# Making the combined forms of x earlier in a SwiGLU feed-forward of a two-layer trunk

## The chip, the cores and the metric

One Trainium2 chip, one core. The metric is the device time of one execution of the whole program in microseconds; the profile is of one execution on that core.

## What is computed

The trunk has two layers over x (512 tokens x 1024). Each layer runs: feed-forward, mixer (an mLSTM in the first layer, a gated MLP in the second), feed-forward, gated embedding; after each of them stands `x = LayerNorm(alpha * x + sublayer(x))`. So there are four feed-forwards, and the change touches these alone:

```python
D_MODEL = 1024; SEQ = 512; DEPTH = 2; FFN_HIDDEN = 2816

def swiglu_ffn(x, w_gu, w_d):
    g, u = jnp.split(x @ w_gu, 2, axis=-1)
    return (jax.nn.silu(g) * u) @ w_d

for i in range(DEPTH):
    x = layer_norm(DN_ALPHA * x + 0.5 * swiglu_ffn(x, ffn1_wgu[i], ffn1_wd[i]), ln_g[i, 0], ln_b[i, 0])
    # ... the mixer of this layer and its norm ...
    x = layer_norm(DN_ALPHA * x + 0.5 * swiglu_ffn(x, ffn2_wgu[i], ffn2_wd[i]), ln_g[i, 2], ln_b[i, 2])
    # ... the gated embedding and its norm ...
```

## The kernel before

Every float32 operand of a product is held as two parts, a high one (`xh`, `whi`, `fhi`) and the rest (`xl`, `wlo`, `flo`), and each product is three matmuls: high by high (L388), and the two mixed ones (L389, L390). ScalarE makes a high part with a copy (L275, L393, L942), VectorE the rest with a subtraction (L284, L394, L945); for some weights the rest is made by ScalarE and an accumulating DMA from GpSimd's queue (L281, L282).

A feed-forward goes through its 22 blocks of 128 hidden columns in six chunks, `FFN_CHUNKS = [2, 4, 4, 4, 4, 4]`. In the chunks c = 0 and 1 the up products are plain: for each of the 2n values of i one product of all eight blocks of x with 128 columns (tile `fps`; the first three, `sup`, are begun before x is complete), then `sg` (ScalarE, SiLU) for even i and `h` (VectorE, L1193) for odd i. From chunk 2 on (`UP_FROM = 2`) the up products use a seven-product scheme (Strassen's, in Winograd's form): four products of quarters of x and of the weights become seven products, r = 0 to 6, of sums of quarters (tile `ups`). Meanwhile the previous chunk's down products run in the same scheme (class `Group`, tile `gps`, added to `xt` by VectorE at L762 and L764).

The seven products need sums of x's quarters, and `UpForms` makes them once in each feed-forward by a list of ten steps, of which `formed.step()` runs the next. A quarter is half of x's blocks by half of the tokens. The steps, in order, with the names of the trace:

1. `x22`: high and low part of a quarter added into two half tiles `x_a` (L1001, two instructions)
2. `x_f`, tile b: the same of a second quarter (L1001)
3. `t3`: b = x_a - b (L1013, two)
4. `x_f`, tile c: the same of a third quarter, which lies in the last 256 tokens (L1001)
5. c = b + c (L1027)
6. `split_t2`: `t_whi` by ScalarE (L393), `t_wlo` by VectorE (L394)
7. `t1`: x_a = x_a - c (L1017, two)
8. `split_t1`: two `t` by ScalarE (L393), two by VectorE (L394)
9. `x21`: `x_d` (L1001, two), of a quarter in the last 256 tokens
10. `t4`: x_d = x_d - c (L1038, two)

The first three need the first 256 tokens alone. What is left, the split of t3 into `xh` and `xl` and that of t4 into `t_f`, is made by `formed.last` in the first products of chunk 2.

There is no scheduler: each engine runs its instructions in the order in which the program writes them, and waits on semaphores where data or a buffer is not there. Weights go through rings of buffers that `W.release()` refills (ScalarE's copy, VectorE's or the DMA's rest, SyncE's next load). After the first feed-forward, chunk 0 and the first values of i in chunk 1 also hold `run_affine`, two VectorE instructions over all of `xt` (L756, L757).

In chunk 2 the product r = 2 adds onto the bank of r = 0, and r = 4 onto that of r = 2. So each of them waits until ScalarE has copied the bank (`take`, L1086, tile `us`).

Of the kernel before, what the change touches and what calls it, by code (L numbers as in the profile page):

```python
# [357 lines left out]
def hybrid_trunk(ctx: ExitStack, tc, x, p, ln_g, ln_b, ffn1_wgu, ffn1_wd, ffn2_wgu, ffn2_wd,  # L358
# [9 lines left out]
    def stage_pool(name, bufs=1):  # L368
        return tc.tile_pool(name=name, bufs=bufs, side="left", reuse_waits="tile")
# [30 lines left out]
    def up_bank(name, hold=False):  # L400

        i = next(i for i in up_order if i not in up_held)
        up_order.remove(i)
        up_order.append(i)
        bank = ps_up.tile([P, 512], F32, name=name, tag=f"up{i}")
        if hold:
            up_held.add(i)
            return i, bank
        return bank
# [60 lines left out]
    FFN_CHUNKS = [2, 4, 4, 4, 4, 4]  # L470
    LAST = len(FFN_CHUNKS) - 1
    UP_FROM = 2
    FORM_AT = 2
    turn_p = []

    def ffn_weights(wgu, wd, name, ple=False):
# [233 lines left out]
    class Norm:  # L710
# [18 lines left out]
        def prepare(self, t):  # L729
            mv = small.tile([P, 2], F32, name="mv", tag="mv")  # L730
            vec.bn_aggr(mv, self.st[t])
            rs = small.tile([P, 2], F32, name="rs", tag="rs")
            vec.tensor_scalar(rs[:, 0:1], mv[:, 1:2], EPS, None, op0=OP.add)
            pool.tensor_tensor(rs[:, 1:2], rs[:, 0:1], eps_pow, op=OP.pow)
            self.rs[t] = mv[:, 0:1], rs[:, 1:2]
# [115 lines left out]
    def up(ps, w, t0=0, t1=SEQ, hooked=()):  # L851

        for kb in range(KB):
            if kb in hooked:
                run_hook()
            mm3(ps[:, t0:t1], [a[:, kb] for a in w], xs(kb, t0, t1), kb == 0, kb == KB - 1)

    def up_staged(first=False):

        banks = [up_bank("sup") for _ in range(3)]  # L860
        ws = []

        def low_last(w, ps, t0, t1):

            for k0, kbs in ((0, range(KB // 2)), (1, range(KB // 2, KB))):
                for kb, a in ([(kb, a) for a in w for kb in kbs] if first else [(kb, a) for kb in kbs for a in w]):
                    mm(ps[:, t0:t1], a[:, kb], xh[:, kb, t0:t1], start=kb == 0 and a is w[0], stop=False)
            if not first and not t0:
                run_hook()
            for kb in range(KB):  # L870
                mm(ps[:, t0:t1], w[0][:, kb], xl[:, kb, t0:t1], start=False, stop=kb == KB - 1)

        for i, ps in enumerate(banks):
            w = W.take()
            ws.append(w)
            if i:
                up(ps, w, 0, 256, (((0,), (2, 7)) if first else ((), (0, 3)))[i - 1])
                continue
            if not first:
                run_hook()  # L880
            low_last(w, ps, 0, 256)
        low_last(ws[0], banks[0], 256, SEQ)
        for ps, w in zip(banks[1:], ws[1:]):
            up(ps, w, 256, SEQ)
        return banks
# [224 lines left out]
    def ffn(layer, k, rows, late, prepare=None):  # L1110
        with stage_pool("forms", 2) as fpool, stage_pool("quarters", Q_BUFS) as qpool, \
                stage_pool("hpool", 2) as hpool, stage_pool("tforms") as tpool:
            name = (layer, k)
            W.open_raw(name, qpool, Q_BUFS)
            banks = deque(up_staged((layer, k) == (0, 0)))

            def project():
                if banks:
                    return banks.popleft()
                ps = up_bank("fps")  # L1120
                up(ps, W.take())
                return ps

            def halves(a):
                return a[:, :SEQ], a[:, SEQ:]

            group, hs, norm, formed = None, [], None, None

            def up_products(c, n, h):
                nonlocal norm  # L1130
                for s in range(7 * n // 2):
                    b, r = s // 7 * 2, s % 7
                    if r == 0:
                        pair = UpPair(formed, None if h is None else h[:, b:b + 2])
                    pair.product(r)
                    W.clock += 1
                    group.add()
                    if r == 5 and h is None:
                        pair.parts = [W.spare(name).rearrange("p (b t) -> p b t", b=2) for _ in range(2)]
                        hs.extend([a[:, e] for a in pair.parts] for e in range(2))  # L1140
                    if r == 6:
                        pair.gated(1, pair.part[2], pair.part[3])
                    pair.take(r)
                    group.finish_form()
                    W.lows()
                    if c == UP_FROM and s in formed.last:
                        formed.last[s]()
                    W.release()
                    pair.gate(r)
                    W.form_ahead(3)  # L1150
                    if s % 2:
                        group.product()
                        W.release(kind="rows")
                        group.form(True)
                    if s == 12 and h is not None:
                        next_group = Group(h, fpool)
                        next_group.form()
                    if c == LAST and b == n - 2:
                        if r == 2:
                            W.open("rowsx", late, 1)  # L1160
                        elif r == 4:
                            norm = Norm(layer, k)
                group.add()
                W.lows()
                return next_group if h is not None else None

            for c, n in enumerate(FFN_CHUNKS):
                if c < LAST:
                    h = hpool.tile([P, 4, SEQ], F32, name="h", tag="h")[:, :n]
                elif prepare is not None:  # L1170
                    prepare()
                if c == UP_FROM - 1:
                    formed = UpForms(tpool, late)
                W.apart = c >= UP_FROM
                if c >= UP_FROM:
                    next_group = up_products(c, n, h if c < LAST else None)
                    if c < LAST:
                        next_group.form()
                    group.add()
                    group = next_group  # L1180
                for i in range(2 * n if c < UP_FROM else 0):
                    b = i // 2
                    ps = project()
                    W.clock += 2
                    if group is not None and i:
                        group.add()
                    if i % 2 == 0:
                        sg = tmp_tile("sg")
                        sca.activation(sg, ps, AF.Silu)
                        W.release()  # L1190
                    else:
                        hf = h[:, b] if c < LAST else tmp_tile("hf")
                        vec.scalar_tensor_tensor(hf, sg, 0.5, ps, op0=OP.mult, op1=OP.mult)  # L1193
                        if c == LAST:
                            hs.append(halves(W.spare(name)))
                            split(*hs[b], hf)
                        W.release()
                        run_hook()
                    if group is not None and i < 7:
                        group.product()  # L1200
                        W.release(kind="rows")
                        group.form()
                    if c == 1 and i < 3:
                        run_affine()
                    if formed is not None and i >= FORM_AT:
                        formed.step()
                        formed.step()
                    if c and i == 6:
                        next_group = Group(h, fpool)
                        next_group.form()  # L1210
                if c < UP_FROM and c:
                    group = next_group
                    group.form()
                if c == UP_FROM - 1:
                    while formed.steps:
                        formed.step()
                if c == 0:
                    group = Group(h, fpool, c == 0)
                    group.form()
                    group.form()  # L1220
                if c == 0:
                    run_affine()
            W.apart = False
            return down(hs, False, norm, lazy=layer == 0, defer=prepare is not None)
# [727 lines left out]
```

## Time and profile before

| | us |
|---|---|
| median of 3 runs | 2213.9 |
| the runs | 2211.8, 2213.9, 2218.28 |
| the profiled execution | 2217.81 |
| its span, first to last instruction | 2216.1 |
| TensorE busy in it | 2179.8 (98%) |
| VectorE busy in it | 1762.2 (80%) |
| ScalarE busy in it | 1209.0 (55%) |
| mean granted TensorE clock | 0.994 |

Times within the trace count from the first instruction. Matmuls overlap, so TensorE's busy time is not TensorE at its peak; where it waits stands in the waits and the timeline. The four feed-forwards begin at about 0, 764, 1172 and 1800 us. Times of a place below are those of the second one, the second feed-forward of the first layer.

### The profile page before, as it was taken

Reading aid. Unit: us, or ns where it says so; the run is one execution under the profiler, and the core shown is the slowest. Engines: PE = TensorE matmul, PEld = TensorE weight load, DVE = VectorE, ACT = ScalarE, POOL = GpSimd, SP = SyncE. Lnnn points to the kernel's source line nnn. Section 1 sums busy time; section 2 is a strip of 40 time slices with the busy share of each in tenths; the row PEclk is TensorE's granted clock in tenths of the full one; section 3 lists DMA queues with packets and bytes.
Section 4 is the critical chain, followed back from the end, with each engine's and each line's share of the span. In section 5 each row is a group of like instructions: output and inputs, shape, how many; then the busy total and the mean of one; then the engine's idle time right before and its main releaser. Section 6 shows DMA issues by size and latency. Waiting matters only on the chain.

```text
span 2216.1 us, 32537 instructions
## 1 busy us (share of the span) xinstructions
PE 2179.8 (98%) x12821; PEld 1928.9 (87%) x12821; DVE 1762.2 (80%) x2532; ACT 1209.0 (55%) x1668; POOL 227.2 (10%) x279
## 2 busy tenths in 40 slices
PE   9999999999999999999999999999999999999998
PEld 8899997888888888999888799997888888899987
DVE  5898877777776779888886998877788768888887
ACT  3566656464646435666445466655345453666542
POOL 1011100011101101111000011110001100111100
PEclk9999999999999999999999999999999999999999
DMA  6587764376847435787532587753437733777651
GB/s 189 149 200 189 176 160 125 82 161 127 164 109 161 124 112 133 193 200 169 164 124 68 140 199 185 179 142 135 142 77 152 163 122 114 173 183 180 140 181 58
DMA packets 228097, 329.46 MB, mean 149 GB/s; under 512 B 9140, under 2 KB 163892, under 8 KB 227944
## 3 DMA queue, kind: packets, MB, share of 16 engines
q1 hardware_dynamic: 169104, 211.83, 29.1%
q0 software_dynamic: 52224, 100.86, 27.3%
q10 hardware_dynamic: 6616, 14.69, 2.0%
q8 instruction: 101, 1.65, 0.3%
q14 instruction: 52, 0.43, 0.1%
HBM read 224.58 MB, written 2.11 MB: 102 GB/s over the span
## 4 chain that ended last, share of the span: by engine, by line
PE 80%; DVE 10%; ACT 4%; issue 3%; DMA 2%; SPq 0%; POOL 0%; DVEq 0%; ACTq 0%; POOLq 0%
PE ups L388 8%; PE ups L390 8%; PE ups L389 8%; PE gps L388 7%; PE gps L389 7%; PE gps L390 7%; PE dps L389 2%; PE dps L390 2%; PE dps L388 2%; DVE wlo L284 2%; ACT whi L275 1%; PE gups L388 1%; PE vps L388 1%; PE zps L388 1%; PE zps L390 1%
## 5 line engine op out<-in xcount | busy, mean ns | idle before, releaser
L275 ACT ACTIVATE whi<-wbox 128x1024 fp32r<-128x1024 f32 x224 | 235.9, 1054 | 229.6 <-DVE wbox L141 101.6
L388 PE MATMUL ups<-xh,whi 128*128 128x256 f32 x1024 | 293.1, 286 | 11.5 <-ACT us L1086 11.5
L390 PE MATMUL ups<-xh,wlo 128*128 128x256 f32 x1024 | 293.0, 286 | 3.3 <-DMA wlo<-wbox 3.3
L389 PE MATMUL ups<-xl,whi 128*128 128x256 f32 x1024 | 292.6, 286 | 0.0
L275 ACT ACTIVATE whi<-wraw 128x1024 fp32r<-128x1024 f32 (+1 forms) x212 | 217.2, 1046 | 97.2 <-DVE wraw L119 22.6
L388 PE MATMUL gps<-whi,fhi 128*128 128x512 f32 x644 | 253.2, 393 | 1.3 <-ACT wlo L281 0.7
L390 PE MATMUL gps<-whi,flo 128*128 128x512 f32 x644 | 251.8, 391 | 1.7 <-DVE flo L945 1.7
L389 PE MATMUL gps<-wlo,fhi 128*128 128x512 f32 x644 | 252.3, 392 | 0.0
L282 POOL DMA_DIRECT2D wlo<-wbox x144 | 122.4, 850 | 1098.1 <-ACT wlo L281 772.4
L764 DVE TENSOR_TENSOR xt<-xt,gps 128x512 f32<-128x512 f32 x302 | 195.2, 681 | 26.7 <-PE gps L390 26.4
L388 PEld LDWEIGHTS ups<-xh,whi 128*128 128x128 f32 x1024 | 199.3, 195 | 15.4 <-ACT us L1086 13.2
L284 DVE TENSOR_TENSOR wlo<-wraw,whi 128x1024 fp32r<-128x1024 f32 (+1 forms) x140 | 167.7, 1214 | 46.0 <-ACT whi L275 45.2
L390 PEld LDWEIGHTS ups<-xh,wlo 128*128 128x128 f32 x1024 | 199.2, 195 | 4.1 <-DMA wlo<-wbox 4.1
L389 PEld LDWEIGHTS ups<-xl,whi 128*128 128x128 f32 x1024 | 199.4, 195 | 2.3
L275 ACT ACTIVATE whi<-wquarter 128x1024 fp32r<-128x1024 f32 (+1 forms) x140 | 135.3, 966 | 80.7 <-DVE wquarter L119 28.9
L281 ACT ACTIVATE wlo<-wbox 128x1024 fp32r<-128x1024 f32 x144 | 150.3, 1044 | 0.0
L390 PEld LDWEIGHTS gps<-whi,flo 128*128 128x128 f32 x644 | 120.9, 188 | 29.7 <-DVE flo L945 3.0
L388 PEld LDWEIGHTS gps<-whi,fhi 128*128 128x128 f32 x644 | 121.3, 188 | 25.8 <-ACT wlo L281 1.9
L389 PEld LDWEIGHTS gps<-wlo,fhi 128*128 128x128 f32 x644 | 121.3, 188 | 21.5
L945 DVE TENSOR_TENSOR flo<-h,fhi 128x512 fp32r<-128x512 f32 (+1 forms) x140 | 88.9, 635 | 57.5 <-ACT fhi L942 56.8
L290 DVE TENSOR_TENSOR wlo<-wquarter,whi 128x1024 fp32r<-128x1024 f32 x104 | 126.7, 1218 | 0.0
L388 PE MATMUL fps<-xh,whi 128*128 128x512 f32 x288 | 112.2, 390 | 0.0
(365 smaller groups left out, 5828.0 us busy)
## 6 DMA issues: line engine op xcount, KB each, us to landing
wlo<-wbox POOLq DMA_DIRECT2D x144, 512.0 KB, 5.7
wbox<-in_ffn_wgu_dram SPq DMA_DIRECT2D x128, 512.0 KB, 4.9
wquarter<-in_ffn_wd_dram SPq DMA_DIRECT2D x64, 512.0 KB, 5.9
wraw<-in_ml_w_in_dram SPq DMA_DIRECT2D x24, 1024.0 KB, 5.9
wlo<-wraw POOLq DMA_DIRECT2D x48, 512.0 KB, 6.4
wraw<-in_ffn_wgu_dram SPq DMA_DIRECT2D x15, 1024.0 KB, 5.9
wraw<-in_gm_w_in_dram SPq DMA_DIRECT2D x15, 1024.0 KB, 5.5
wraw<-in_ffn_wgu_dram SPq DMA_DIRECT2D x17, 512.0 KB, 4.6
```

Source lines behind the costliest of these rows:

```text
L275: self.nc.scalar.activation(hi[:, s], src[:, s], AF.Copy)
L281: self.nc.scalar.activation(lo[:, s], src[:, s], AF.Copy, scale=-1.0)
L282: self.nc.gpsimd.dma_start(lo[:, s], src[:, s], accum_op=OP.add)
L284: self.nc.vector.tensor_sub(lo[:, s], src[:, s], hi[:, s].bitcast(F32))
L290: self.nc.vector.tensor_sub(lo, src, hi.bitcast(F32))
L388: mm(ps, st[0], mv[0], start=start, stop=False, skip_group_check=more)
L389: mm(ps, st[0], mv[1], start=False, stop=False, skip_group_check=more)
L390: mm(ps, st[1], mv[0], start=False, stop=stop, skip_group_check=more)
L764: vec.tensor_add(dst, dst, ps)
L945: vec.tensor_sub(lo, src, hi.bitcast(F32))
```

## The change

`UpForms` is built at the start of chunk 0 instead of chunk 1, and one step is run at each i from 1 on, in both chunks. Chunk 0 has four values of i and so runs the steps 1 to 3; chunk 1 has eight and runs the steps 4 to 10, one each at i = 1 to 7. Before, chunk 1 alone ran them, two each at i = 2 to 6.

```diff
-    FORM_AT = 2
...
-                if c == UP_FROM - 1:
+                if c == UP_FROM - 2:
                     formed = UpForms(tpool, late)
...
                     if c == 1 and i < 3:
                         run_affine()
-                    if formed is not None and i >= FORM_AT:
-                        formed.step()
+                    if formed is not None and (i and c == UP_FROM - 2 or i > 0 and c == UP_FROM - 1):
                         formed.step()
```

One line is taken out near the head of the program, so lines behind it have a number lower by one in the changed kernel (L1001 becomes L1000). The instructions are the same ones; TensorE, GpSimd and SyncE have the same order as before. Three places in the second feed-forward show what moves.

VectorE in chunk 0, ahead of and behind its last `h`; before:

```order
L284 TENSOR_TENSOR wlo<-wquarter,whi 128x512
L284 TENSOR_TENSOR wlo<-wraw,whi 128x1024
L1193 SCALAR_TENSOR_TENSOR h<-sg,fps 128x512
L945 TENSOR_TENSOR flo<-h,fhi 128x256 x2
L756 TENSOR_TENSOR xt<-xt,gb 128x1024
L757 TENSOR_TENSOR xt<-xt,gb 128x1024
```

VectorE at the same place now (`x_f_7565` is tile b):

```order
L284 TENSOR_TENSOR wlo<-wquarter,whi 128x512
L1000 TENSOR_TENSOR x_a<-xh,xl 128x512 x2
L284 TENSOR_TENSOR wlo<-wraw,whi 128x1024
L1000 TENSOR_TENSOR x_f_7565<-xh,xl 128x1024
L1192 SCALAR_TENSOR_TENSOR h<-sg,fps 128x512
L1012 TENSOR_TENSOR x_f_7565<-x_a,x_f_7565 128x512 x2
L944 TENSOR_TENSOR flo<-h,fhi 128x256 x2
L755 TENSOR_TENSOR xt<-xt,gb 128x1024
L756 TENSOR_TENSOR xt<-xt,gb 128x1024
```

The steps 1, 2 and 3 have come in from chunk 1, one to each i.

VectorE at the end of chunk 1 and the start of chunk 2, around the last `h`; before (`x_f_7632` is tile c):

```order
L284 TENSOR_TENSOR wlo<-wbox,whi 128x1024
L1001 TENSOR_TENSOR x_d<-xh,xl 128x512 x2
L1038 TENSOR_TENSOR x_d<-x_d,x_f_7632 128x512 x2
L945 TENSOR_TENSOR flo<-h,fhi 128x512
L762 SCALAR_TENSOR_TENSOR xt<-xt,gps 128x512 x2
L1193 SCALAR_TENSOR_TENSOR h<-sg,fps 128x512
L284 TENSOR_TENSOR wlo<-wquarter,whi 128x1024
L945 TENSOR_TENSOR flo<-h,fhi 128x512
L394 TENSOR_TENSOR xl<-x_f_7631,xh 128x4x256
```

VectorE at the same place now (`x_f_7566` is tile c, `x_f_7565` tile b):

```order
L284 TENSOR_TENSOR wlo<-wbox,whi 128x1024
L1000 TENSOR_TENSOR x_d<-xh,xl 128x512 x2
L944 TENSOR_TENSOR flo<-h,fhi 128x512
L761 SCALAR_TENSOR_TENSOR xt<-xt,gps 128x512 x2
L1192 SCALAR_TENSOR_TENSOR h<-sg,fps 128x512
L284 TENSOR_TENSOR wlo<-wquarter,whi 128x1024
L1037 TENSOR_TENSOR x_d<-x_d,x_f_7566 128x512 x2
L944 TENSOR_TENSOR flo<-h,fhi 128x512
L394 TENSOR_TENSOR xl<-x_f_7565,xh 128x4x256
```

The subtraction of step 10 has gone behind the last `h`, ahead of the next `flo` and of `xl`.

ScalarE in chunk 1, around `t_whi` of step 6; before:

```order
L1189 ACTIVATE sg<-fps 128x512
L275 ACTIVATE whi<-wquarter 128x512
L275 ACTIVATE whi<-wraw 128x1024
L275 ACTIVATE whi<-wbox 128x1024
L942 ACTIVATE fhi<-h 128x256
L393 ACTIVATE t_whi<-x_f_7632 128x1024
L275 ACTIVATE whi<-wbox 128x1024
```

ScalarE at the same place now:

```order
L393 ACTIVATE t_whi<-x_f_7566 128x1024
L1188 ACTIVATE sg<-fps 128x512
L275 ACTIVATE whi<-wquarter 128x512
L275 ACTIVATE whi<-wraw 128x1024
L275 ACTIVATE whi<-wbox 128x1024
L941 ACTIVATE fhi<-h 128x256
L275 ACTIVATE whi<-wbox 128x1024
```

`t_whi` has gone ahead of the `sg` of i = 4; on VectorE c = b + c (step 5) stands one i ahead of `t_wlo` (step 6), where both stood in one i before.

## The prediction

> **What bounds the kernel now.** The page comes first, for the engine that sets the time:
>
> ```profile
> span 2216.1 us, 32537 instructions
> PE 2179.8 (98%) x12821; PEld 1928.9 (87%) x12821; DVE 1762.2 (80%) x2532; ACT 1209.0 (55%) x1668; POOL 227.2 (10%) x279
> ```
>
> TensorE is idle for 36.3 us in all (2216.1 - 2179.8). The change neither adds nor removes a matmul, so it can win only such idle time, or clock. The view of TensorE's waits, and its timeline around the change (start, length, instruction, idle time before it and what ended that), say where it lies:
>
> ```profile
> PE ups L388 <- ACT us L1086: 12.8, 7, 3.3
> 104.57 0.39 PE L390 MATMUL gps<-whi,flo 128*128 128x512 f32 x1
> 106.49 0.39 PE L388 MATMUL ups<-xh,whi 128*128 128x256 f32 x1 [1.54 <-ACT us L1086]
> 835.39 0.47 PE L388 MATMUL gps<-whi,fhi 128*128 128x512 f32 x1 [0.23 <-ACT wlo L281]
> 849.24 0.50 PE L390 MATMUL gps<-whi,flo 128*128 128x512 f32 x1 [0.56 <-DVE flo L945]
> 852.24 0.39 PE L388 MATMUL ups<-t_whi,whi 128*128 128x256 f32 x1 [0.44 <-ACT us L1086]
> 860.35 0.39 PE L389 MATMUL gps<-wlo,fhi 128*128 128x512 f32 x1
> 860.58 0.39 PE L390 MATMUL gps<-whi,flo 128*128 128x512 f32 x1
> 864.28 0.39 PE L388 MATMUL ups<-xh,whi 128*128 128x256 f32 x1 [3.31 <-ACT us L1086]
> 1272.83 0.58 PE L388 MATMUL ups<-xh,whi 128*128 128x256 f32 x1 [3.33 <-ACT us L1086]
> 1900.95 0.58 PE L388 MATMUL ups<-xh,whi 128*128 128x256 f32 x1 [3.31 <-ACT us L1086]
> ```
>
> Seven waits for `us` cost 12.8 us, the largest item, and all sit at the start of chunk 2. The long one, before product r = 4, comes once in each feed-forward. A matmul of 512 columns follows the last after 0.23 us (860.35 to 860.58), so r = 4 could have gone at 860.81 and went at 864.28: 3.47 us lost, 0.16 more than the idle time named. Counted so, the second feed-forward loses 0.39 + 0.72 + 0.60 + 3.47 = 5.2 us here, the first 1.7.
>
> Then the clock, in windows (TensorE busy, granted clock, DMA share):
>
> ```profile
> 335.14 0.50 PE L389 MATMUL dps<-wlo,wquarter 128*128 128x512 f32 x1 [1.60 <-DVE wlo L290]
> 336.40:339.70 3.30, 3.30 (x9) 0.50 0.93 336
> 860.00:864.20 4.20, 0.97 (x5) 1.00 0.87 166
> 865.40:868.80 3.40, 3.40 (x18) 0.50 1.06 250
> 1271.60:1278.40 6.80, 5.57 (x26) 0.50 1.03 212
> 1899.70:1906.40 6.70, 5.45 (x25) 0.50 1.02 217
> ```
>
> Behind each wait of 3.3 us TensorE runs at half clock, and loses half of its busy time there: 1.7, 2.8 and 2.7 us, 7.2 together. After 1.60 us of waiting it happened once as well (336.40); after the 1.54 us of the first feed-forward it did not.
>
> Why is `us` late? The timelines of ScalarE and VectorE, followed back from r = 4:
>
> ```profile
> 863.65 0.58 ACT L1086 ACTIVATE us<-ups 128x512 f32<-128x512 f32 x1
> 856.82 1.06 ACT L275 ACTIVATE whi<-wbox 128x1024 fp32r<-128x1024 f32 x1 [3.69 <-DVE wbox L149]
> 855.56 1.23 DVE L149 TENSOR_TENSOR wbox<-wbox 128x1024 f32<-128x1024 f32 x1
> 851.07 0.64 ACT L942 ACTIVATE fhi<-h 128x512 fp32r<-128x512 f32 x1 [2.79 <-DVE h L1193]
> 850.29 0.68 DVE L1193 SCALAR_TENSOR_TENSOR h<-sg,fps 128x512 f32<-128x512 f32 x1
> 842.07 0.39 PE L390 MATMUL fps<-xh,wlo 128*128 128x512 f32 x1
> 818.00:844.00 26.00, 25.56 (x119) 20.84 (x118) 24.50 (x33) 9.20 (x13) 0.88 (x1) 1.00 0.53 158
> ```
>
> From 856.82 ScalarE works without a pause until that `us`; it had waited for VectorE's sum of weights (L149). VectorE in turn made the last `h` of chunk 1 at 850.29, though its `fps` was complete at 842.46: it is 7.8 us behind. The windows row (TensorE, weight loads, VectorE 24.50, ScalarE 9.20 of 26 us) shows why: VectorE is full in the second half of chunk 1, where the ten steps stand. The bound at this place is VectorE's queue, not TensorE.
>
> **The change part by part.** What the steps cost there, and a wait among them:
>
> ```profile
> 818.12 1.28 DVE L1001 TENSOR_TENSOR x_a<-xh,xl 128x512 f32<-128x512 f32 x2
> 819.32 1.22 DVE L1001 TENSOR_TENSOR x_f<-xh,xl 128x1024 f32<-128x1024 f32 x1
> 824.32 1.29 DVE L1013 TENSOR_TENSOR x_f<-x_a,x_f 128x512 f32<-128x512 f32 x2
> 832.32 1.06 ACT L393 ACTIVATE t_whi<-x_f 128x1024 fp32r<-128x1024 f32 x1 [6.48 <-DVE x_f L1027]
> 833.42 1.23 DVE L394 TENSOR_TENSOR t_wlo<-x_f,t_whi 128x1024 fp32r<-128x1024 f32 x1 [1.13 <-ACT t_whi L393]
> 835.18 1.04 ACT L275 ACTIVATE whi<-wquarter 128x1024 fp32r<-128x1024 f32 x1
> 847.29 1.29 DVE L1038 TENSOR_TENSOR x_d<-x_d,x_f 128x512 f32<-128x512 f32 x2
> ```
>
> Neighbours overlap by 0.08 us (818.12 + 1.28 against 819.32), which I take off each.
>
> 1. Steps 1 to 3 leave chunk 1: 1.20 + 1.14 + 1.21 = 3.5 us ahead of the last `h`.
> 2. `t_wlo` stands one i behind c = b + c instead of right behind it, so ScalarE makes `t_whi` meanwhile, inside the 6.48 us that it idles: the 1.13 us go.
> 3. Step 10 goes behind the last `h`: 1.2 us earlier for `h`, given back to all that is behind it (`flo`, `xl`, L149).
> 4. On the other side, `wlo<-wquarter` of i = 5 will come so early that it waits for ScalarE's `whi<-wquarter` (835.18 before, held up behind `t_whi`); I take 0.5 us off, an estimate.
>
> So the last `h` comes 3.5 + 1.1 + 1.2 - 0.5 = 5.3 us earlier, near 845, still after its `fps`. L149 comes 4.1 us earlier. Behind the last `h` VectorE also waited 0.45 us for `xh` (L393), which ScalarE now has in time, since it gets its `h` 5.3 us sooner: 4.6. The chain of ScalarE from there to `us` is of fixed length (863.65 - 856.82 = 6.8 us), so r = 4 may start at 864.28 - 4.6 = 859.7. TensorE itself, without the three small waits (1.7 us), is there at 859.1. The gain is 4.6 us of the 5.2, with 0.6 of a wait left. Its ends: 3.5 (step 10's subtraction is paid in full and nothing but the steps is won) and 5.2 (no wait is left). Three feed-forwards: 13.8.
>
> The three steps land in chunk 0, on VectorE:
>
> ```profile
> 34.99 0.69 DVE L1193 SCALAR_TENSOR_TENSOR h<-sg,fps 128x512 f32<-128x512 f32 x1 [3.27 <-PE fps L390]
> 42.51 0.69 DVE L284 TENSOR_TENSOR wlo<-wquarter,whi 128x512 fp32r<-128x512 f32 x1 [4.46 <-ACT whi L275]
> 784.58 1.23 DVE L284 TENSOR_TENSOR wlo<-wraw,whi 128x1024 fp32r<-128x1024 f32 x1 [1.60 <-ACT whi L275]
> 788.47 0.69 DVE L1193 SCALAR_TENSOR_TENSOR h<-sg,fps 128x512 f32<-128x512 f32 x1 [2.67 <-PE fps L390]
> 795.98 0.69 DVE L284 TENSOR_TENSOR wlo<-wquarter,whi 128x512 fp32r<-128x512 f32 x1 [2.19 <-ACT whi L275]
> ```
>
> `x_a` (1.2) goes into the idle 1.60, `x_f` (1.1) into the 2.67. Only t3 (1.2) delays what is behind it, `flo` and the sums to the next idle time, 2.19 us, which takes it up. In the first feed-forward 3.27 and 4.46 us stand at the same two places. Cost: 0. If that cover were gone, t3 would be paid, 1.2 us each time, up to 4.8 in all. No load is issued by a step; SyncE's loads wait for VectorE's `wlo`, which stay in place in chunk 0 and come earlier in chunk 1.
>
> The first feed-forward has no `run_affine`, so its VectorE is less late and another limit is near:
>
> ```profile
> 87.87 1.06 ACT L275 ACTIVATE whi<-wbox 128x1024 fp32r<-128x1024 f32 x1 [0.22 <-PE fps L389]
> ```
>
> There ScalarE waits for TensorE itself. The gain is between 0 and the 1.7 us lost; I take 1.5, since VectorE's order is relieved in the same way.
>
> The clock: with 0.6 us of wait left, far below the 1.54 after which it stayed up, the halving has no ground: 7.2 us. [...]
>
> Sum: 13.8 + 1.5 + 7.2 = 22.5 us. The profiled execution took 2217.81 us, so 2195.3. It is 3.9 above the median of the runs, 2213.9; part of that may be the clock, which then cannot be won again. I put 2194.
>
> **The rivals.**
>
> Clock unchanged: the halving comes from something other than the waits (DMA is at its fullest there too, 1.06 and 1.03) and stays. Then 15.3 us: 2217.8 - 15.3 = 2202.5. For it speaks that the wait of 1.54 us was followed by nothing and that of 1.60 us by half clock, so that the wait alone does not decide; against it that three of the three long waits have the half clock right behind them. [...]
>
> Half a gain: a load or ScalarE sets L149 or r = 4 once VectorE is earlier. If 2 us per feed-forward are won, a wait of 2.6 to 3 us is left at three places and the halving mostly stays: 6 + 1.5 + 2 = 9.5, some 2208. For it: ScalarE's wait on TensorE at 87.87. Against it: no idle time of VectorE between 845 and 850 names a DMA.
>
> [...]
>
> **How the numbers follow.** 0.3% of 2213.9 is 6.6 us, about what a measurement of this kernel can tell from no change: faster is below 2207.3, slower above 2220.5. Chances: my forecast 0.68, clock unchanged 0.14, half a gain 0.12, slower 0.06. Faster: 0.68 + 0.14 and 0.05 of the half gain, 0.87; same: the other 0.07; slower 0.06. The forecast's own range goes from 2189 (5.2 three times, 1.7 and the clock are 24.5, from the median) to 2200 (3.5 three times and the clock). The range for 8 in 10 adds the unchanged clock with its lower ends: 2187 to 2206.
>
> **What would show it.** Right: `x_a` in chunk 0 without a wait of TensorE there; no idle time before `t_wlo`; the last `h` of chunk 1 some 5 us earlier; the wait of 3.3 us before r = 4 under 1 us; full clock in chunk 2's start. Wrong: that wait still above 2 us, with ScalarE waiting for something other than L149; a new wait of TensorE in chunk 0 or 1; or the half clock at those places without a wait.

## The result, and the profile after

The changed kernel takes 2193.99 us (median of 4 runs, 2193.04 to 2194.74), the kernel before beside it 2214.55 us (median of 4, 2211.80 to 2218.28): a ratio of 0.9906 [0.9889, 0.9923], 20.6 us. The profiled execution of the changed kernel took 2193.39 us. The page's span and engines:

```profile
span 2191.7 us, 32537 instructions
PE 2170.3 (99%) x12821; PEld 1922.0 (88%) x12821; DVE 1760.5 (80%) x2532; ACT 1208.1 (55%) x1668; POOL 226.3 (10%) x279
```

The instructions are as many as before, and VectorE's busy time is the same within 2 us. TensorE is idle for 21.4 us (2191.7 - 2170.3) where it was 36.3, and is 9.5 us less busy for the same matmuls, most of which is clock (1.6 and 6.4 us by the counts below). TensorE's longest waits (what waited, for what: us in all, times, the longest):

```profile
PE dps L389 <- DVE wlo L290: 4.8, 4, 1.6
PE ups L390 <- DMA wlo<-wbox: 3.9, 6, 1.0
...
PE sup L866 <- ACT xh L639: 1.1, 2, 0.8
```

The 12.8 us of `ups <- us` are gone from the list. TensorE's timeline at the start of chunk 2, with r = 4 of the four feed-forwards:

```profile
105.01 0.39 PE L388 MATMUL ups<-xh,whi 128*128 128x256 f32 x1
855.56 0.39 PE L390 MATMUL gps<-whi,flo 128*128 128x512 f32 x1
855.91 0.39 PE L388 MATMUL ups<-xh,whi 128*128 128x256 f32 x1
1258.54 0.39 PE L388 MATMUL ups<-xh,whi 128*128 128x256 f32 x1
1878.38 0.39 PE L388 MATMUL ups<-xh,whi 128*128 128x256 f32 x1
```

No row has a bracket, so none waited long enough for the view to name it. In the second feed-forward r = 4 starts 0.35 us after the matmul ahead of it, against 3.70 before and 0.23 between matmuls that wait for nothing. The clock at the same places, and after the wait of 1.6 us (windows: TensorE busy, clock, DMA share):

```profile
336.40:339.70 3.30, 3.30 (x16) 1.00 1.05 402
857.00:863.00 6.00, 6.00 (x48) 1.00 1.04 209
1259.00:1265.00 6.00, 6.00 (x50) 1.00 1.07 213
1879.00:1885.00 6.00, 6.00 (x50) 1.00 1.07 215
```

All run at 1.00. So do the 3.3 us at 336.40, although the wait of 1.6 us ahead of them (the first row of the waits) is still there: the half clock that stood there before did not recur, without that wait having gone. VectorE in chunk 0, in chunk 1, and from the last `h` on:

```profile
780.02 1.28 DVE L1000 TENSOR_TENSOR x_a<-xh,xl 128x512 f32<-128x512 f32 x2
781.71 1.23 DVE L284 TENSOR_TENSOR wlo<-wraw,whi 128x1024 fp32r<-128x1024 f32 x1 [0.40 <-ACT whi L275]
782.85 1.22 DVE L1000 TENSOR_TENSOR x_f<-xh,xl 128x1024 f32<-128x1024 f32 x1
785.60 0.69 DVE L1192 SCALAR_TENSOR_TENSOR h<-sg,fps 128x512 f32<-128x512 f32 x1 [1.52 <-PE fps L390]
786.20 1.29 DVE L1012 TENSOR_TENSOR x_f<-x_a,x_f 128x512 f32<-128x512 f32 x2
793.11 0.69 DVE L284 TENSOR_TENSOR wlo<-wquarter,whi 128x512 fp32r<-128x512 f32 x1 [1.23 <-ACT whi L275]
...
821.38 1.22 DVE L394 TENSOR_TENSOR t_wlo<-x_f,t_whi 128x1024 fp32r<-128x1024 f32 x1
829.91 1.22 DVE L284 TENSOR_TENSOR wlo<-wquarter,whi 128x1024 fp32r<-128x1024 f32 x1
841.26 0.68 DVE L1192 SCALAR_TENSOR_TENSOR h<-sg,fps 128x512 f32<-128x512 f32 x1
843.00 1.28 DVE L1037 TENSOR_TENSOR x_d<-x_d,x_f 128x512 f32<-128x512 f32 x2
847.19 1.22 DVE L149 TENSOR_TENSOR wbox<-wbox 128x1024 f32<-128x1024 f32 x1
```

The idle stretches in chunk 0 are now 0.40, 1.52 and 1.23 us, where they were 1.60, 2.67 and 2.19: each gave up about one step. `t_wlo` follows its neighbour without a pause. This feed-forward starts 2.87 us earlier than before, because of what was won ahead of it; without that, the last `h` is 6.16 us earlier (850.29 against 841.26) and L149 is 5.50 (855.56 against 847.19). ScalarE at the same places:

```profile
817.63 1.06 ACT L393 ACTIVATE t_whi<-x_f 128x1024 fp32r<-128x1024 f32 x1 [2.17 <-DVE x_f L1026]
827.11 1.04 ACT L275 ACTIVATE whi<-wquarter 128x1024 fp32r<-128x1024 f32 x1
848.45 1.06 ACT L275 ACTIVATE whi<-wbox 128x1024 fp32r<-128x1024 f32 x1 [4.34 <-DVE wbox L149]
855.29 0.58 ACT L1085 ACTIVATE us<-ups 128x512 f32<-128x512 f32 x1
```

From 848.45 to 855.29 are 6.84 us, and from 856.82 to 863.65 they were 6.83: the chain is the same, begun earlier.

Where the 24.4 us between the two spans went, from matmuls of the same number in the order. I cut each feed-forward into the stage from the second matmul of chunk 1 (0.23 us behind the first) to the first of r = 4, and the rest up to the next such place:

| us | FF 1 | FF 2 | FF 3 | FF 4 |
|---|---|---|---|---|
| stage to r = 4, before | 71.47 | 75.79 | 75.79 | 75.78 |
| stage to r = 4, after | 69.90 | 70.29 | 70.33 | 70.33 |
| rest, before | 682.00 | 332.76 | 552.34 | 306.43 |
| rest, after | 680.61 | 332.29 | 549.51 | 304.58 |

The stages give 1.57 + 5.50 + 5.46 + 5.45 = 18.0 us, which are waits; the rests give 1.39 + 0.47 + 2.83 + 1.85 = 6.5 us, where the half clock was. In the first rest the half clock at 336.40 was about 1.6 us, and a new wait at 142.6 took 0.5 back.

### The profile page after: what moved, and what is told of

The parts are those of the page before. It is cut to its first block, busy times and chain, and to the rows that moved or that the text cites. A ratio compares the mean times of both kernels' runs of the same rounds, so it can differ in the third digit from the quotient of the medians.

```text
span 2191.7 us, 32537 instructions
## 1 busy us (share of the span) xinstructions
PE 2170.3 (99%) x12821; PEld 1922.0 (88%) x12821; DVE 1760.5 (80%) x2532; ACT 1208.1 (55%) x1668; POOL 226.3 (10%) x279
## 4 chain that ended last, share of the span: by engine, by line
PE 78%; DVE 11%; issue 4%; ACT 4%; DMA 3%; SPq 0%; POOL 0%; DVEq 0%; ACTq 0%; POOLq 0%
PE ups L390 7%; PE ups L388 7%; PE ups L389 7%; PE gps L388 6%; PE gps L389 6%; PE gps L390 6%; DMA wlo<-wbox 2%; PE dps L389 2%; PE dps L390 2%; PE dps L388 2%; DVE wlo L290 2%; PE fps L388 2%; PE fps L389 1%; PE fps L390 1%; ACT whi L275 1%
## 5 line engine op out<-in xcount | busy, mean ns | idle before, releaser
L390 PE MATMUL ups<-xh,wlo 128*128 128x256 f32 x1024 | 290.3, 284 | 3.2 <-DMA wlo<-wbox 3.2
L390 PE MATMUL gps<-whi,flo 128*128 128x512 f32 x644 | 251.4, 390 | 0.0
L390 PEld LDWEIGHTS ups<-xh,wlo 128*128 128x128 f32 x1024 | 196.2, 192 | 4.3 <-DMA wlo<-wbox 4.2
L390 PEld LDWEIGHTS gps<-whi,flo 128*128 128x128 f32 x644 | 120.9, 188 | 26.9
```

The lines of the kernel that those rows point to most:

```text
L390: mm(ps, st[1], mv[0], start=False, stop=stop, skip_group_check=more)
```

## The experiments

Unless it says otherwise, a time is the median with its range, and a ratio is to the kernel before. The first four kernels ran beside 16 runs of the kernel before (median 2215.07), the next four beside 13 (2215.66), the last beside 7 (2215.23). In the first three and the last, a table gives how many steps are run at (chunk, i).

**The first three steps alone.** The rest stay in pairs as before.

```diff
+    FORM_STEPS = {(0, 1): 1, (0, 2): 1, (0, 3): 1, (1, 3): 1, (1, 4): 2, (1, 5): 2, (1, 6): 2}
...
-                    if formed is not None and (i and c == UP_FROM - 2 or i > 0 and c == UP_FROM - 1):
+                    for _ in range(FORM_STEPS.get((c, i), 0)):
                         formed.step()
```

> The kernel before with steps 1 to 3 alone moved into chunk 0; steps 4 to 10 stay at the i where they were (4 at i = 3, 5 and 6 at 4, 7 and 8 at 5, 9 and 10 at 6). Theory, VectorE's queue: L149 comes 3.5 us earlier, so of the 5.2 us that TensorE loses per feed-forward some 1.7 are left, most of it as one wait before r = 4; the 1.13 us before t_wlo stay. The time is 2214.5 - 3 x 3.5 - 1.5 and 3 to 7 us of clock, 2196 to 2200. Rival, the spacing of the steps (one to each i, no handshake with ScalarE): little is won here, 2208 to 2213.

2202.94 us (2202.00 to 2203.33), 0.9945 [0.9930, 0.9959]. The stage to r = 4 is 71.47, 72.25, 72.25, 72.25 us: 3.54 less than before in the last three feed-forwards, which is what the three steps took of VectorE (3.5), and nothing in the first. TensorE and VectorE in the timeline:

```profile
827.97 1.23 DVE L394 TENSOR_TENSOR t_wlo<-x_f,t_whi 128x1024 fp32r<-128x1024 f32 x1 [1.13 <-ACT t_whi L393]
858.84 0.38 PE L388 MATMUL ups<-xh,whi 128*128 128x256 f32 x1 [2.32 <-ACT us L1086]
```

The wait for `t_whi` is unchanged at 1.13 us, and r = 4 still waits 2.3. The full time was above the 2196 to 2200 that I expected, though the stages did what the steps cost (I had also counted 1.5 us for the first feed-forward and 3 to 7 of clock); 10.6 us of waits were won (3 x 3.54) and 12.1 us of time. Two of its three waits of 2.32 us were still followed by half clock, at 1263.7 and 1888.4, one stretch of 3.4 us each.

**The spread alone.** On the kernel before: nothing moves to chunk 0, but `t_wlo` stands one i behind c = b + c and step 10 behind the last `h`.

```diff
+    FORM_STEPS = {(1, 2): 2, (1, 3): 2, (1, 4): 1, (1, 5): 2, (1, 6): 2, (1, 7): 1}
...
-                    if formed is not None and i >= FORM_AT:
-                        formed.step()
+                    for _ in range(FORM_STEPS.get((c, i), 0)):
                         formed.step()
```

> The kernel before with the order of chunk 1 alone changed: step 5 at i = 4, 6 and 7 at 5, 8 and 9 at 6, 10 at 7; steps 1 to 4 stay in chunk 1 where they were. Theory, VectorE's queue: only the wait of 1.13 us before t_wlo goes, L149 comes 1.1 us earlier, a wait of some 2.5 us before r = 4 and most of the half clock stay: 2209 to 2212. Rival, the spacing of the steps: most of the gain is here, 2196 to 2201.

2208.65 us (2207.82 to 2211.37), 0.9973 [0.9961, 0.9984], just under the 2209 to 2212 expected. The stage is 70.83 us in the first feed-forward (0.64 less) and 73.83 in the others (1.96 less, where I had expected 1.1). In the timeline:

```profile
860.51 0.58 PE L388 MATMUL ups<-xh,whi 128*128 128x256 f32 x1 [3.40 <-ACT us L1087]
```

The wait before r = 4 is as long as ever: the spread also removed the small waits ahead of it, so TensorE arrives earlier and waits for the rest. 3.54 and 1.96 make 5.50, the stage gain of the whole change: in the last three feed-forwards its two halves add up. In the first they don't (0 and 0.64 against 1.57); I did not trace the limit there further.

**Step 10 ahead of the last `h`.** The changed kernel, with steps 9 and 10 both at i = 6.

```diff
+    FORM_STEPS = {(0, 1): 1, (0, 2): 1, (0, 3): 1, (1, 1): 1, (1, 2): 1, (1, 3): 1, (1, 4): 1, (1, 5): 1, (1, 6): 2}
```

> The changed kernel with step 10 put back ahead of the last h, at i = 6. Theory, L149 decides: it stands behind both in either order, so its time stays; the last h comes 1.2 us later (near 842.5 with the shift of this run) and still in time for the banks of r = 0 and r = 2: 2193 to 2196. Rival, the last h decides: 1.2 us of wait per feed-forward come back, 2198 to 2199.

2194.69 us (2194.20 to 2198.78), 0.9912 [0.9897, 0.9927], not told apart from the changed kernel. The profiled execution is the one of 2198.78 us; it has a stretch of half clock at 1489.9 us, behind a wait of `dps`, which is outside the stage. The traces can tell the stages apart:

```profile
842.42 0.68 DVE L1193 SCALAR_TENSOR_TENSOR h<-sg,fps 128x512 f32<-128x512 f32 x1
847.69 1.23 DVE L149 TENSOR_TENSOR wbox<-wbox 128x1024 f32<-128x1024 f32 x1
856.41 0.39 PE L388 MATMUL ups<-xh,whi 128*128 128x256 f32 x1 [0.48 <-ACT us L1086]
```

The last `h` is 1.16 us later than in the changed kernel, step 10's own time, and L149 0.50; r = 4 waits 0.48 us. So the place of step 10 is worth 0.5 us in a feed-forward: neither nothing, nor the whole 1.2.

**The half clock alone.** On the kernel before: 28 matmuls into a free bank, whose result nobody reads, stand ahead of r = 4 in the last three feed-forwards. The wait stays; TensorE is not idle in it.

```diff
+            def fill_pe(count):
+                at = next(j for j in up_order if j not in up_held)
+                bank = ps_up.tile([P, 512], F32, name="fill", tag=f"up{at}")
+                for _ in range(count):
+                    mm(bank[:, :256], xh[:, 0, :P], xh[:, 0, 256:], start=True, stop=True, skip_group_check=True)
...
+                    if c == UP_FROM and s == 4 and (layer, k) != (0, 0):
+                        fill_pe(28)
                     pair.product(r)
```

> The kernel before with 28 further matmuls of 128x256 (products of xh with itself, into a free bank, read by nobody) ahead of r = 4 in chunk 2 of the second, third and fourth feed-forward; they fill 3.4 us in which TensorE waited. Theory, the waits bring the half clock: r = 4 starts when it did, and the three stretches of half clock behind it are gone: 2214.5 - 7 = 2206 to 2209. Rival, the half clock has another cause (the DMA load, the products themselves): same stretches as before, 2213 to 2217.

2212.29 us (2210.72 to 2214.60), 0.9986 [0.9976, 0.9995]: 2.8 us, an interval from 1.1 to 5.3. The stage is 71.48 and three times 75.79, as before. TensorE, then the windows behind r = 4:

```profile
858.60 3.51 PE L1133 MATMUL fill<-xh 128*128 128x256 f32 x28
862.09 0.38 PE L388 MATMUL ups<-xh,whi 128*128 128x256 f32 x1
```

```profile
862.20:868.90 6.70, 6.70 (x53) 1.00 1.08 210
1268.70:1275.40 6.70, 6.70 (x52) 1.00 1.07 207
1895.20:1901.90 6.70, 6.70 (x52) 1.00 1.07 213
```

Full clock in all three, with the DMA share at 1.07 and 1.08, as high as in the slowed stretches of before (1.06, 1.03, 1.02). So at these three places TensorE's idle time brought the half clock, and the DMA load did not. What it is worth came out below what I expected (2206 to 2209).

**One and three more subtractions ahead of the last `h`.** The changed kernel, step 9 run twice (the diff), and four times (`range(4)`): 1.2 and 3.6 us more of VectorE.

```diff
             def x21():
-                for i, s in enumerate(halves):
-                    joined(d[i], 1, 0, s)
+                for _ in range(2):
+                    for i, s in enumerate(halves):
+                        joined(d[i], 1, 0, s)
```

> The changed kernel with 1.2 us more of VectorE's work ahead of the last h in chunk 1 of every feed-forward: step 9 is run twice (it writes the same values again). Theory, the length of VectorE's queue ahead of L149: TensorE's stretch from chunk 1 to r = 4, 70.3 us in the changed kernel, becomes 71.3 to 71.5, and the wait before r = 4 some 1.2 us; 2194.0 + 3 x 1.1 + 0 to 1, 2197 to 2199. Rival, the forms were not ready in time and the early steps mended that: nothing changes, 2193 to 2195.

> The changed kernel with step 9 run four times, 3.6 us more of VectorE's work ahead of the last h. Theory, VectorE's queue: the stretch to r = 4 becomes 73.6 to 73.9 us, that is, what moving steps 1 to 3 had won is lost again, and stretches of half clock come back in some runs; 2194.0 + 10.5 + 1 to 4, 2205 to 2209. Rival, readiness of the forms: 2193 to 2196.

2198.55 us (2197.32 to 2199.52), 0.9925 [0.9908, 0.9942], and 2210.12 us (2208.78 to 2211.28), 0.9976 [0.9967, 0.9986]. The first is as expected; the second lies above its 2205 to 2209, which had left out the first feed-forward, whose stage grew by 1.9 us. In the last three the stage grows from 70.3 to 71.5 and to 73.9 us, by 1.2 and 3.6: one to one. TensorE in the first of the two, then in the second, and the second's windows:

```profile
857.16 0.39 PE L388 MATMUL ups<-xh,whi 128*128 128x256 f32 x1 [1.16 <-ACT us L1086]
```

```profile
861.54 0.39 PE L388 MATMUL ups<-xh,whi 128*128 128x256 f32 x1 [3.57 <-ACT us L1086]
```

```profile
863.10:866.40 3.30, 3.30 (x18) 0.50 1.03 253
1269.30:1272.60 3.30, 3.30 (x17) 0.50 1.06 248
1893.90:1897.20 3.30, 3.30 (x16) 0.50 1.01 225
```

Waits of 1.16 us left the clock up at all three places, waits of 3.57 us brought it down at all three. Against its own runs of the kernel before, the second gains 5.5 us where the changed kernel gained 20.6, 15.1 less. The stages account for 12.7 of them (1.9 + 3 x 3.6), so some 2.4 us are left for the half clock, whose three stretches of 3.4 us would cost 3 x 1.7 = 5.1 if half of the time were lost in them: again less than that.

**Twice the work in chunk 0.** The changed kernel, each of the three steps there with one more addition of the same size, 3.5 us in all.

```diff
             self.steps = [
-                x22, lambda: joined(b, 0, 1), t3, lambda: joined(c, 0, 0), lambda: vec.tensor_add(c, b, c),
+                lambda: (x22(), x22()), lambda: (joined(b, 0, 1), joined(b, 0, 1)), lambda: (x22(), t3()), lambda: joined(c, 0, 0), lambda: vec.tensor_add(c, b, c),
                 split_t2, t1, split_t1]
```

> The changed kernel with the work in chunk 0 doubled: step 1 runs twice with itself, step 2 twice, and step 1 once more ahead of step 3 (same values), 3.5 us more of VectorE there. Theory, chunk 0 has idle time: the changed kernel's VectorE still idles 0.40, 1.52 and 1.23 us at the three places there, 3.15 in all, so at most 0.4 us come through to chunk 1 and the stretch to r = 4 is 70.3 to 70.8: 2194 to 2196. Rival, the cover is used up: all 3.5 us come through, stretch 73.8, 2205 to 2208.

2197.94 us (2197.45 to 2200.13), 0.9924 [0.9910, 0.9939], 3 to 4 us more than the changed kernel (2.8 less gain against its own runs of before, 4.0 in the times), and above the 2194 to 2196 expected. The stage to r = 4 is 69.90 in the first feed-forward, as in the changed kernel, and 71.4 in the others, 1.1 more:

```profile
782.03 2.49 DVE L1000 TENSOR_TENSOR x_f<-xh,xl 128x1024 f32<-128x1024 f32 x2
784.43 0.68 DVE L1192 SCALAR_TENSOR_TENSOR h<-sg,fps 128x512 f32<-128x512 f32 x1
792.69 0.69 DVE L284 TENSOR_TENSOR wlo<-wquarter,whi 128x512 fp32r<-128x512 f32 x1 [0.78 <-ACT whi L275]
...
817.93 0.47 PE L388 MATMUL gps<-whi,fhi 128*128 128x512 f32 x1 [1.18 <-DVE xt L761]
```

The idle 0.40 and 1.52 us are used up, but of the 1.23 us before `wlo<-wquarter` 0.78 are left. So 0.40 + 1.52 + 0.45 = 2.4 of the 3.5 us were covered, and the other 1.1 came out as a wait of TensorE in chunk 1. My expectation took the 1.23 us for cover; but VectorE waits there for a `whi` that ScalarE copies from VectorE's own result (L114), so what delays VectorE delays the end of that wait as well. In the changed kernel this copy still waited for TensorE (idle 0.81 us, ended by `gps`, L390), which is where the usable 0.45 us came from; here L114 ends its wait:

```profile
792.03 0.63 ACT L275 ACTIVATE whi<-wquarter 128x512 fp32r<-128x512 f32 x1 [1.93 <-DVE wquarter L114]
```

**A shorter chain of ScalarE, and the later steps one i later.** First the changed kernel with one up product's rest less made by ScalarE and the accumulating DMA; then, on top of that, step 4 at i = 1, the steps 5 to 7 at i = 3 to 5, 8 and 9 at 6, and 10 at 7.

```diff
-UP_BY_DMA = (1, 3, 4, 5, 6)
+UP_BY_DMA = (1, 3, 5, 6)
```

The second kernel has this as well:

```diff
+    FORM_STEPS = {(0, 1): 1, (0, 2): 1, (0, 3): 1, (1, 1): 1, (1, 3): 1, (1, 4): 1, (1, 5): 1, (1, 6): 2, (1, 7): 1}
```

> The changed kernel with the weights' rest for r = 4 in the first pair of every chunk made by VectorE instead of by ScalarE and an accumulating DMA (UP_BY_DMA without 4). It asks what comes next: TensorE's waits on such DMAs are 3.9 us in all in the changed kernel and 1 to 2 of them new. If these DMAs are the next limit, 2191 to 2193; if VectorE, at 80% busy, is, the 1.2 us that it gets in each of four chunks and four feed-forwards make new waits, 2196 to 2210.

> A version that may be better: the run dma_less with step 5 at i = 3 instead of 2, and with it 6 at 4, 7 at 5, 8 and 9 at 6 (10 stays at 7). In the changed kernel TensorE still waits 0.3 us for VectorE's xt at i = 4, ahead of which steps 4 and 5 stand. If VectorE's place in the queue is what is left there, that wait goes and the stretch from chunk 1 to r = 4, 70.2 us in dma_less, becomes 69.9, TensorE's own time; 2193 to 2195, no more than 1 us better than the changed kernel. If the handshake for t_whi comes back (step 6 one i behind step 5 as in the changed kernel, so it should not), 71 us and 2197.

2194.34 us (2192.29 to 2196.30), 0.9906 [0.9891, 0.9921], and 2193.36 us (2192.66 to 2195.30), 0.9899 [0.9883, 0.9916]. Neither is told apart from the changed kernel; the first lies between the two ranges that I had written down, so it bears out neither. The gap before r = 4 falls from 0.35 to 0.23 us in both, and in the second the stage is 69.77 us in all four feed-forwards: nothing waits in it, TensorE alone sets its length. The largest items of TensorE's waits in that kernel:

```profile
PE ups L390 <- DMA wlo<-wbox: 5.1, 8, 1.1
PE dps L389 <- DVE wlo L290: 5.0, 4, 1.6
```

The stage that the change is about has at most 0.56 us a feed-forward left (70.33 - 69.77), some 2 in all, and the time shows at most part of that. What TensorE still waits for lies elsewhere.

## Why the prediction came out, and which of its terms were off

**The bound** was VectorE's queue in the second half of chunk 1, as the prediction said, and it is shown: 3.5 us of work taken out ahead of the last `h` brought r = 4 forward by 3.54 us, and 1.2 and 3.6 us put in set it back by 1.2 and 3.6. ScalarE's chain behind L149 kept its length and only moved.

**The wait in the last three feed-forwards** was charged at 4.6 us and measured 5.5, above the upper end of 5.2. The term that failed is the 0.5 us for ScalarE's `whi<-wquarter` at i = 5. I had expected VectorE to run into it; ScalarE had itself come forward, with `t_whi` no longer right ahead of this copy, and made `whi` at 827.11, complete 1.8 us before VectorE wanted it at 829.91. So the last `h` came 6.16 us earlier and not 5.3: 3.5 + 1.1 + 1.2 = 5.8, and 0.3 that I did not trace. L149 came 5.50 earlier and not 4.6, and the gap before r = 4 was 0.13 us more than between other matmuls, not 0.6. The upper end of 5.2 also fell short, as it was counted from the gaps that I had listed at the start of chunk 2 alone: the stage held 6.0 us over what TensorE needs (75.79 - 69.77).

**Step 10's place** was counted 1.2 us earlier for `h` and given back behind it. Both are seen; the 0.45 us that VectorE no longer waits for `xh` is the difference, and the move is worth 0.5 us.

**Chunk 0** cost nothing, as predicted, and by the rows named: 1.60 to 0.40, 2.67 to 1.52, 2.19 to 1.23. The first feed-forward won 1.57 us, with 1.5 forecast.

**The clock** was charged at 7.2 us. That it went with the waits, and not with the DMA, is shown by the filled waits: clock 1.00 at all three places, at DMA shares of 1.07 and 1.08. The size was too large, and the step that failed is "loses half of its busy time". Behind r = 4, matmuls of 256 columns start 0.213 us apart at half clock and 0.119 at full clock, so the half clock took 44% of their time. Counted from matmuls of the same number, the three stretches cost 1.50, 2.44 and 2.42 us, 6.4 together, in the changed kernel and with the filled waits alike.

The three rests together give less, 0.47 + 2.83 + 1.85 = 5.2 us, chiefly because TensorE, when it comes earlier, meets other waits. In the second feed-forward 0.78 of the 1.5 us won are lost again at the first of these two matmuls (changed kernel), and 0.40 at the second:

```profile
890.90 0.39 PE L390 MATMUL ups<-xh,wlo 128*128 128x256 f32 x1 [0.51 <-DMA wlo<-wbox]
894.17 0.39 PE L390 MATMUL ups<-t_f,wlo 128*128 128x256 f32 x1
```

The first waits for a `wlo` made by the accumulating DMA; what held the second is not named. With VectorE making one such `wlo` instead (the run without 4 in `UP_BY_DMA`) both delays are gone, and that rest is 331.42 us, not 332.29. In all, the waits of that kind went from 3.3 to 3.9 us.

With the wait kept and the half clock removed, the medians differ by only 2.8 us (1.1 to 5.3). The reason lies in what I charged it from: the profiled execution of before had a mean clock of 0.994, and of the 36 runs of the same kernel beside the experiments 28 had 0.996 or 0.997; those with 0.997 took 2213.8 us on average, those with 0.994 2217.3. In the traces 0.994 goes with 20.5 us at half clock ahead of the last matmul (before), 0.996 with 13.7 (the spread alone), 0.997 with 6.8 and 10.2 (the first three steps alone, three more subtractions). So by this estimate most executions had a third to two thirds of the half clock of the one that I charged it from, and I took only 1.3 us off for that.

So the sum, 22.5 us, is made of a wait that was 2.7 us too small (15.3 against 18.0) and a clock that was too large, by 2.0 us against the profiled execution and by 4.4 against the medians. Its last step, from 2195.3 to 2194, rested on the clock's part in the profiled execution; the time came out there because the two errors were of opposite signs, and that 2194 meets 2193.99 so closely is luck. With the measured terms, 18.0 + 2.8 = 20.8 us, beside 20.6 in the runs.

**The rivals.** Clock unchanged: excluded, the windows are at 1.00. Half a gain: excluded, no wait of 2 us is left. Slower, with step 10 now ahead of `flo`, `xl` and L149: excluded; L149 came 5.50 us earlier.

## What to carry to other kernels

When an engine works through its queue in order and is nearly full ahead of the result that others wait for (VectorE here, 24.50 of 26 us), work moved out of that stretch can come back to the waiting engine one to one (here 3.54 us for 3.5), until that engine's own work is the limit (here 69.77 us). Moved only to just behind the result, work can bring less (here 0.5 of 1.2 us), where something behind it is waited for too. Count idle time as cover only where it ends on something that doesn't itself depend on the idle engine: of 1.23 us that ended on a copy of VectorE's own result, 0.45 could be used. And charge a clock penalty from several executions, not from the profiled one, since the mean clock differs between runs of one kernel (here 0.994 to 0.997 in 36).

## What the runs showed of the hardware

All of this is measured in the traces of this case. Ahead of the last matmul the half clock came in stretches of 3.41 or 6.83 us, and in the trace of before they start on one grid: 336.3, 865.4, 1271.6 and 1899.6 us lie 529.1, 406.2 and 628.0 us apart, which is 155.0, 119.0 and 184.0 times 3.413. In the run with the first three steps alone the waits before r = 4 in the last three feed-forwards are all of 2.32 us. The first of them fell across two intervals of such a grid, with TensorE idle for 1.03 and 1.29 us in them, and was followed by nothing; the second fell into one, with 2.30 us idle, and half clock followed (intervals of the grid: TensorE busy, clock, DMA share):

```profile
854.13:857.55 3.42, 2.39 (x11) 1.00 0.80 153
857.55:860.96 3.41, 2.12 (x17) 1.00 0.94 156
1260.32:1263.73 3.41, 1.11 (x5) 1.00 1.00 191
```

Of the places before r = 4, those where TensorE lost 3.5 to 3.7 us were followed by half clock in 9 of 9 cases (before, the spread alone, three more subtractions), those with 2.5 us in 2 of 3 (the first three steps alone), those with 1.7 to 2.0 us in 0 of 4 (the first feed-forward of before, of the first three steps alone, of the filled waits, and of three more subtractions), those with 1.3 us in 0 of 3 (one more subtraction). Elsewhere a wait of 1.6 us before `dps` was followed by it at 336.3 in before, and at 1487.7 to 1489.9 in three others (twice the work in chunk 0, step 10 ahead of the last `h`, the later steps), but not in the changed kernel, which ran at 1.00 at 336.40 behind the same wait of 1.60 us.

Counted by intervals of the grid instead of waits, the eleven traces agree. Of the intervals that ran at full clock, all 14 in which TensorE was idle for 1.72 us or more were followed by half clock (1.72, 2.30, 2.08 and 2.01 us in before), one of the nine with 1.60 or 1.61 us was, and none with 1.56 us or less. Of the intervals at half clock, those with 0.92 us or more idle were followed by a second one in 3 of 3 cases (1.25 and 1.31 us in before), those with 0.49 us or less in 0 of 15.
